# Reordering the step from the output projection to the gate/up products in a one-core encoder layer

## The chip, the core and the metric

The kernel runs on one core of a Trainium2 chip. The metric is the device time of one execution in microseconds. Five engines matter: PE (TensorE, the matrix products and transposes), ACT (ScalarE), DVE (VectorE), POOL (GpSimd) and SP (SyncE); the last two mostly issue DMA transfers. Each engine works through its own queue in the order in which the program wrote it, and waits at an instruction until the semaphores named there are reached.

## What is computed

One layer of a bidirectional encoder on 512 tokens of width 2048, all in float32. The part of it around the change is the end of the mixer, the second RMSNorm and the first half of the feed-forward block:

```
mixed = concat([attn_out, gla_out]) @ w_out
x = x + mixed
h = rmsnorm(x, ffn_norm_w)             # x * rsqrt(mean(x*x) + eps) * w
x = x + (silu(h @ w_gate) * (h @ w_up)) @ w_down
return rmsnorm(x, final_norm_w)
```

`w_out` is 2048x2048; `w_gate` and `w_up` are 2048x5632; `w_down` is 5632x2048.

## The kernel before

Every float32 product is made of products of two rounded halves, a high part and a low part, so one tile product is several matmuls.

**Output projection.** A job per 512 output columns (c = 0 to 3) runs over 16 k-tiles and accumulates four PSUM banks, one for each 128 tokens (`run_job`, L303 to L305). Before the job of c it has the residual tiles x1[c] loaded. When the job ends, `evac_out(c)` (L1033) adds the banks to x1[c] on DVE (L1038); for c = 3 in eight adds of 256 columns, the left halves of all four banks first, then the right halves. The rest is a generator appended to the queue `urgent`: `rest()` for c < 3, `rest_last()` (L1060) for c = 3. Each call of `run_urgent` (L235) runs the first generator in that queue up to its next `yield`, so what stands between two yields is emitted at the place of the call, on all engines at once.

**What the generators do.** `weighted` (L358) transposes four 128x128 blocks on PE into one PSUM bank (L362), and ACT copies that bank out with the norm's weight (L364). `pair_operands` (L1009) makes the seven token operands of a pair of k-tiles from two such copies: four subtractions and additions on DVE (L1014, L1017), then seven casts on ACT (L1026) and seven subtractions on DVE (L1014). `keep` (L1044) squares x1 on ACT with a row sum (L409) and stores x1 to DRAM from POOL's queue (L1047). `rstd_of` (L318) turns the sums into the reciprocal root: a scale, ACT's Ln and Exp (L323, L324), and four small operations of DVE. `rows_of` (L330) spreads the root along the tokens by matmuls with a broadcast column (L334) and an ACT copy (L337).

**Gate/up products.** `Feed.run` (L1340) walks over units (one of w_gate or w_up, 256 columns) of four pieces each (four k-tiles, 512 KB of weights). A piece needs sums of weight blocks (DVE, L1208 to L1211), a low part of the raw blocks (ACT L1186, then an accumulating DMA of POOL, L1187; the high part is L1188), and the split of the sums (ACT L1225, DVE L1226). They are emitted one to three pieces ahead, by `split`, `sums` and `part`. `products` (L1249) then multiplies: seven products (two matmuls each, one for each of the piece's pairs of k-tiles) of 512 columns with the high weights (L1278), then fourteen of 256 columns with the low weights (L1284). Products 0 to 5 accumulate over the unit in three double banks `pd`; product 6 in a single bank of the two called `pe`. The other `pe` bank is what the transposes and the rows get. Those are the eight PSUM banks, and they are the ones that the output projection has just used: a `pd` tile can be written once the adds have read the old banks under it. After a unit's last piece `empty` (L1296) reads each bank with ACT (L1305) and DVE (L1306), and `combine` (L1309) needs the rows for a gate unit (L1327).

The pieces of the first unit (i = 0 to 3) use k-tiles 0 to 15; those of c = 3 are only needed by piece 3. So `rest_last` is spread over pieces 0 to 3 by calls of `run_urgent` in `products` (L1282, L1287) and in `run` (L1346, L1356).

Of the kernel before, what the change touches and what calls it, by code (L numbers as in the profile page):

```python
# [19 lines left out]
OP = mybir.AluOpType  # L20
# [100 lines left out]
def layer(nc, tc, x, attn_norm_w, w_in, rel_table, gw_f, gb_f, gw_b, gb_b, gla_norm_w, w_out,  # L121
# [7 lines left out]
    with tc.manual_schedule(), \  # L129
# [851 lines left out]
        x1 = {}  # L981
# [50 lines left out]

        def evac_out(c):  # L1033
            def f(banks):
                for h in range(2 if c == 3 else 1):
                    a = slice(h * 256, (h + 1) * 256) if c == 3 else slice(0, 512)
                    for t in range(4):
                        dve.tensor_tensor(x1[c][t].t[:, a], x1[c][t].t[:, a], banks[t].t[:, a], op=OP.add)  # L1038
                put(*banks)
                if c < 3:  # L1040
                    load_res(c + 1)
                urgent.append(rest() if c < 3 else rest_last())

            def keep():  # L1044
                for t in range(4):
                    squares(c, t, x1[c], ss2)
                    pool.dma_start(out=xd[4 * c + t], in_=x1[c][t].t)  # L1047

            def rest():
                yield  # L1050
                keep()
                fs_ = {}
                for q in (2 * c, 2 * c + 1):
                    fs_[q] = [weighted(x1[c], k, W_FFN) for k in (2 * q, 2 * q + 1)]
                    yield
                put(*x1.pop(c))
                for q in (2 * c, 2 * c + 1):
                    yield from pair_operands(q, fs_.pop(q))

            def rest_last():  # L1060
                fs_ = {}
                for q in (2 * c, 2 * c + 1):
                    fs_[q] = []
                    for k in (2 * q, 2 * q + 1):
                        fs_[q].append(weighted(x1[c], k, W_FFN))
                        yield
                for q in (2 * c, 2 * c + 1):
                    yield from pair_operands(q, fs_.pop(q))
                keep()
                put(*x1.pop(c))  # L1070
                yield
                dve.tensor_reduce(sum2, ss2.rearrange("p (t c) -> p t c", c=4), op=OP.add,
                                  axis=mybir.AxisListType.X)
                rstd_of(sum2, 4, rstd2, 1.0 / D, scr)
                yield
                rb[2] = rows_of(rstd2)
            return f

# [79 lines left out]
        class Feed(Blocks):  # L1158
# [90 lines left out]
            def products(self, i, more):  # L1249
                st_ = self.sets.pop(i)  # L1250
                u, piece = self.seq[i]
                first, last = piece == 0, piece == self.per - 1
                (rh, rl), (sh, sl) = st_
                if first:
                    self.bank = {}
                if last:
                    groups = ((0, 1), (2, 3), (4, 5), (6,))
                elif first:
                    groups = (tuple(range(7)),)
                else:  # L1260
                    groups = ((0, 1, 5, 2, 3, 4, 6),)
                for group in groups:
                    todo = []
                    for n in group:
                        kind, xn = self.ORDER[n]
                        k = int(kind[1])
                        wh, wl = (rh, rl) if kind[0] == "R" else (sh, sl)
                        if first:
                            if n == 6:
                                self.bank[n] = ps.get()  # L1270
                                self.bank[6, 0] = self.bank[n].t
                            elif n % 2 == 0:
                                d = self.bank[n] = pd.get(F32, [P, 2, 512])
                                self.bank[n, 0], self.bank[n + 1, 0] = d.t[:, 0], d.t[:, 1]
                        o = self.bank[n, 0]
                        for p in range(2):
                            x_ = xs[2 * piece + p][xn]
                            mm(o, wh.t[:, p, k], x_.t.rearrange("p s t -> p (s t)"), start=first and p == 0,  # L1278
                               stop=False, skip_group_check=True)
                            todo.append((o, wl, p, k, x_))  # L1280
                        if i == 0 and n > 4:
                            run_urgent()  # L1282
                    for m, (o, wl, p, k, x_) in enumerate(todo):
                        mm(o[:, 256:512], wl.t[:, p, k], x_.t[:, 0], start=False, stop=last and p == 1,  # L1284
                           skip_group_check=True)
                        if i == 0 and m in (5, 11):
                            run_urgent()  # L1287
                    if last:
                        self.empty(group[0])
                        next(more, None)  # L1290
                        if group[0] == 2:
                            self.part(i + 3)
                for hi, lo in st_:
                    put(hi, lo)
# [45 lines left out]
            def run(self):  # L1340
                for i, (u, q) in enumerate(self.seq):
                    self.load()
                    self.split(i)
                    while 2 * q + 1 not in xs:
                        run_urgent()
                    for _ in range(3 if i in (1, 2) else 0):  # L1346
                        run_urgent()
                    self.sums(i + 1)
                    more = self.sum_steps(i + 2)
                    if q == 0:  # L1350
                        next(self.making, None)
                    else:
                        next(more, None)
                    self.split(i + 1)
                    if i > 3:
                        run_urgent()  # L1356
                    if q < 3:
                        for _ in more:
                            pass
                        if q < 2:  # L1360
                            next(self.making, None)
                        self.part(i + 3)
                        if q == 1:
                            next(self.making, None)
                    if q == 2 and self.sent:
                        put(self.sent)
                        self.sent = None
                    self.products(i, more)
                    if u == len(self.units) - 1:
                        for p in (2 * q, 2 * q + 1):  # L1370
                            put(*xs.pop(p).values())
                        down_start(q)
                    if q == self.per - 1:
                        self.making = self.combine(u)
# [408 lines left out]
```

## Time and profile before

| what | value |
|---|---|
| runs, median (lowest to highest) | 2214.81 us (2214.68 to 2216.66), 3 runs |
| the profiled execution | 2214.19 us, its span 2212.4 us |
| PE busy | 2186.4 us, 99% of the span |
| granted TensorE clock, mean over the span | 0.998 |
| HBM read, written | 246.58 MB, 46.20 MB |
| mean DMA rate | 170 GB/s |

The span is the time from the first to the last instruction of the core; the profiled execution's own time is 1.8 us longer. Start times of rows are counted from the span's start. In a row of the timeline, the first number is the start, the second the length from the start of the first to the end of the last of the instructions that it merges, and the bracket the idle time of the engine before it with what ended it. Matmuls overlap, so a merged row reaches beyond the start of the next one: what PE really takes for a group is the distance between starts.

### The profile page before, as it was taken

How to read it: one execution, taken by the hardware profiler on the slowest of the kernel's cores; microseconds unless marked ns; L12 is line 12 of the kernel's file. 1: busy time of each engine (PE TensorE's matmuls, PEld its weight loads, DVE VectorE, ACT ScalarE, POOL GpSimd, SP SyncE). 2: the span in 40 equal slices, each digit the busy share in tenths (PEclk: the TensorE clock that was granted, in tenths of full speed). 3: DMA queues.
4: the chain of work that ended last, by engine and by line, in shares of the span. 5: the costliest groups of instructions: out<-in, count | busy, mean ns of one | idle time of the engine just before them, and what ended most of it. 6: DMA issues, size and time to landing. Idle time of an engine off the chain costs nothing.

```text
span 2212.4 us, 33114 instructions
## 1 busy us (share of the span) xinstructions
PE 2186.4 (99%) x12374; PEld 1910.5 (86%) x12374; DVE 1565.0 (71%) x2724; ACT 1189.3 (54%) x1990; POOL 326.2 (15%) x349
## 2 busy tenths in 40 slices
PE   9999999999999999999999999999999999999998
PEld 7888888888888887888888888888888899999986
DVE  4366665754455346788888888888888897888777
ACT  5344444444445345666666666666666655555443
POOL 0000000000000011222222222222222200122220
PEclk9999999999999999999999999999999999999999
DMA  6525625242325433888889898898888865687892
GB/s 208 160 72 151 177 81 141 84 133 57 97 66 171 134 105 84 204 193 208 204 194 209 194 212 197 200 210 196 212 193 208 254 185 177 179 199 182 230 370 78
DMA packets 260274, 376.75 MB, mean 170 GB/s; under 512 B 18288, under 2 KB 179744, under 8 KB 260113
## 3 DMA queue, kind: packets, MB, share of 16 engines
q1 hardware_dynamic: 192800, 259.37, 37.6%
q0 software_dynamic: 66128, 114.21, 27.6%
q8 instruction: 97, 1.59, 0.3%
q10 hardware_dynamic: 1184, 1.06, 0.1%
q14 instruction: 65, 0.52, 0.1%
HBM read 246.58 MB, written 46.20 MB: 132 GB/s over the span
## 4 chain that ended last, share of the span: by engine, by line
PE 92%; DVE 3%; DMA 2%; ACT 1%; issue 1%; ACTq 0%; SPq 0%; POOL 0%; POOLq 0%; DVEq 0%
PE pd L1278 21%; PE pd L1284 11%; PE ps L303 5%; PE ps L304 5%; PE ps L305 5%; PE ps L295 5%; PE ps L297 5%; PE ps L296 5%; PE pu L1544 4%; PE pu L1542 4%; PE pu L1543 4%; PE pe L1278 4%; PE pe L1284 2%; PE ps L529 1%; PE pu L304 1%
## 5 line engine op out<-in xcount | busy, mean ns | idle before, releaser
L1278 PE MATMUL pd<-a,b 128*128 128x512 f32 x2112 | 529.6, 393 | 2.4 <-DVE a L1038 1.6
L1278 PEld LDWEIGHTS pd<-a,b 128*128 128x128 f32 x2112 | 380.4, 189 | 69.2 <-issue 2.0
L1284 PEld LDWEIGHTS pd<-a,b 128*128 128x128 f32 x2112 | 288.5, 190 | 21.4
L1284 PE MATMUL pd<-a,b 128*128 128x256 f32 x2112 | 294.9, 282 | 0.0
L202 DVE TENSOR_TENSOR a<-b,a 128x512 fp32r<-128x512 f32 x288 | 193.0, 687 | 138.6 <-ACT a L201 137.2
L1187 POOL DMA_DIRECT2D b<-b x176 | 209.7, 1248 | 535.6 <-ACT b L1186 410.3
L1225 ACT CAST b<-b 128x1024 fp32r<-128x1024 f32 x176 | 185.3, 1053 | 164.1 <-DVE b L1211 136.0
L1544 PE MATMUL pu<-b,a 128*128 128x256 f32 x896 | 255.1, 285 | 6.5 <-DVE a L1507 5.5
L1542 PE MATMUL pu<-b,a 128*128 128x256 f32 x896 | 254.5, 284 | 0.0
L1543 PE MATMUL pu<-b,a 128*128 128x256 f32 x896 | 254.4, 284 | 0.0
L1226 DVE TENSOR_TENSOR b<-b,b 128x1024 fp32r<-128x1024 f32 x176 | 214.9, 1221 | 51.5 <-ACT b L1225 27.7
L201 ACT CAST a<-b 128x512 fp32r<-128x512 f32 x288 | 169.7, 617 | 67.2 <-PE ps L305 22.3
L1544 PEld LDWEIGHTS pu<-b,a 128*128 128x128 f32 x896 | 172.8, 193 | 7.3 <-DVE a L1507 6.2
L1542 PEld LDWEIGHTS pu<-b,a 128*128 128x128 f32 x896 | 172.9, 193 | 0.0
L1543 PEld LDWEIGHTS pu<-b,a 128*128 128x128 f32 x896 | 172.9, 193 | 0.0
L1147 ACT CAST b<-b 128x768 fp32r<-128x768 f32 (+1 forms) x128 | 115.2, 947 | 84.8 <-PE pu L1544 27.4
L1306 DVE TENSOR_TENSOR a<-pd,a 128x512 f32<-128x512 f32 x132 | 91.4, 692 | 95.6 <-ACT a L1305 95.5
L1186 ACT ACTIVATE b<-b 128x768 fp32r<-128x768 f32 x176 | 149.2, 848 | 7.4 <-PE ps L305 5.6
L1152 DVE TENSOR_TENSOR b<-b,b 128x768 fp32r<-128x768 f32 (+1 forms) x128 | 134.4, 1086 | 20.0 <-ACT b L1147 20.0
L1188 ACT CAST b<-b 128x768 fp32r<-128x768 f32 x176 | 145.3, 825 | 0.6 <-PE ps L305 0.6
L1305 ACT COPY a<-pd 128x512 f32<-128x512 f32 x132 | 77.4, 587 | 102.0 <-PE pd L1284 102.0
L1208 DVE TENSOR_TENSOR b<-b 128x512 f32<-128x512 f32 x176 | 120.5, 685 | 0.0
(246 smaller groups left out, 4332.8 us busy)
## 6 DMA issues: line engine op xcount, KB each, us to landing
b<-b POOLq DMA_DIRECT2D x176, 384.0 KB, 5.4
b<-in_w_gate_dram SPq DMA_DIRECT2D x88, 512.0 KB, 4.2
b<-in_w_up_dram SPq DMA_DIRECT2D x88, 512.0 KB, 4.5
b<-in_w_down_dram SPq DMA_DIRECT2D x88, 512.0 KB, 5.6
b<-in_w_in_dram SPq DMA_DIRECT2D x48, 512.0 KB, 3.9
b<-in_w_in_dram SPq DMA_DIRECT2D x94, 256.0 KB, 4.5
b<-in_w_out_dram SPq DMA_DIRECT2D x32, 512.0 KB, 4.9
md<-a POOLq DMA_DIRECT2D x56, 256.0 KB, 8.3
```

The lines of the kernel that those rows point to most:

```text
L201: act.copy(h[2].t, r)
L202: dve.tensor_tensor(h[3].t, r, h[2].f, op=OP.subtract)
L1186: act.activation(lo.t, r, AF.Copy, scale=-1.0)
L1187: pool.dma_start(out=lo.f, in_=r, accum_op=OP.add)
L1188: act.copy(hi.t, r)
L1225: act.copy(hi.t, self.S[i].t)
L1226: dve.tensor_tensor(lo.t, self.S[i].t, hi.f, op=OP.subtract)
L1278: mm(o, wh.t[:, p, k], x_.t.rearrange("p s t -> p (s t)"), start=first and p == 0, stop=False, skip_group_check=True)
L1284: mm(o[:, 256:512], wl.t[:, p, k], x_.t[:, 0], start=False, stop=last and p == 1, skip_group_check=True)
L1542: mm(o, xh[:, t], wh, start=first and h == 0, stop=False, skip_group_check=True)
L1543: mm(o, xh[:, t], wl, start=False, stop=False, skip_group_check=True)
L1544: mm(o, xl[:, t], wh, start=False, stop=last, skip_group_check=True)
```

## The change

The last chunk's residual is added in four adds of 512 columns, a bank each, and each bank is given back after its add. `rest_last` begins with the squares, the store, the sums and the root, in one step; then it makes two transposes and their pair of operands, and again two and a pair; `rows_of` comes last. In the first piece of the first unit, products 0 to 5 get their high and low matmuls first, and the seventh product is opened behind them. The calls of `run_urgent` move: one ahead of the products of piece 0, two within its low matmuls, three ahead of piece 1, two after the second and third product of piece 1, three ahead of piece 2 and one after the second product of piece 2.

```diff
         def evac_out(c):
             def f(banks):
-                for h in range(2 if c == 3 else 1):
-                    a = slice(h * 256, (h + 1) * 256) if c == 3 else slice(0, 512)
-                    for t in range(4):
-                        dve.tensor_tensor(x1[c][t].t[:, a], x1[c][t].t[:, a], banks[t].t[:, a], op=OP.add)
-                put(*banks)
+                for t in range(4):
+                    dve.tensor_tensor(x1[c][t].t, x1[c][t].t, banks[t].t, op=OP.add)
+                    put(banks[t])
...
             def rest_last():
-                fs_ = {}
-                for q in (2 * c, 2 * c + 1):
-                    fs_[q] = []
-                    for k in (2 * q, 2 * q + 1):
-                        fs_[q].append(weighted(x1[c], k, W_FFN))
-                        yield
-                for q in (2 * c, 2 * c + 1):
-                    yield from pair_operands(q, fs_.pop(q))
                 keep()
-                put(*x1.pop(c))
-                yield
                 dve.tensor_reduce(sum2, ss2.rearrange("p (t c) -> p t c", c=4), op=OP.add,
                                   axis=mybir.AxisListType.X)
                 rstd_of(sum2, 4, rstd2, 1.0 / D, scr)
                 yield
+                for q in (2 * c, 2 * c + 1):
+                    fs_ = []
+                    for k in (2 * q, 2 * q + 1):
+                        fs_.append(weighted(x1[c], k, W_FFN))
+                        yield
+                    yield from pair_operands(q, fs_)
+                put(*x1.pop(c))
                 rb[2] = rows_of(rstd2)
...
+                if i == 0:
+                    groups = (tuple(range(6)), (6,))
...
-                        if i == 0 and n > 4:
+                        if (i, n) in ((1, 1), (1, 2), (2, 1)):
                             run_urgent()
...
-                        if i == 0 and m in (5, 11):
+                        if i == 0 and len(group) > 1 and m in (2, 5):
                             run_urgent()
...
-                    for _ in range(3 if i in (1, 2) else 0):
+                    for _ in range((1, 3, 3)[i] if i < 3 else 0):
                         run_urgent()
```

How the instructions stand now is shown at three places. The names are those of the program's buffers: `a_920` to `a_923` are the four residual tiles x1[3], `ps_311` to `ps_314` the last job's banks, `small` holds the sums and the root, `idn` is the identity. Line numbers behind the change are three to five lower (L1278 and L1284 become L1275 and L1281; L1225 and L1226 become L1220 and L1221; L1186 and L1188 become L1181 and L1183).

First place: DVE at the end of the last output job. Before, from the last weight split to the first operation on transposed operands:

```order
L1226 TENSOR_TENSOR b_271_7640<-b_268_7621,b_270_7639 128x1024
L1038 TENSOR_TENSOR a_920_7240<-a_920_7240,ps_311_7248 128x256
L1038 TENSOR_TENSOR a_921_7241<-a_921_7241,ps_312_7249 128x256
L1038 TENSOR_TENSOR a_922_7242<-a_922_7242,ps_313_7250 128x256
L1038 TENSOR_TENSOR a_923_7243<-a_923_7243,ps_314_7251 128x256
L1038 TENSOR_TENSOR a_920_7240<-a_920_7240,ps_311_7248 128x256
L1038 TENSOR_TENSOR a_921_7241<-a_921_7241,ps_312_7249 128x256
L1038 TENSOR_TENSOR a_922_7242<-a_922_7242,ps_313_7250 128x256
L1038 TENSOR_TENSOR a_923_7243<-a_923_7243,ps_314_7251 128x256
```

With the change:

```order
L1221 TENSOR_TENSOR b_271_7640<-b_268_7621,b_270_7639 128x1024
L1036 TENSOR_TENSOR a_920_7240<-a_920_7240,ps_311_7248 128x512
L1036 TENSOR_TENSOR a_921_7241<-a_921_7241,ps_312_7249 128x512
L1036 TENSOR_TENSOR a_922_7242<-a_922_7242,ps_313_7250 128x512
L1036 TENSOR_TENSOR a_923_7243<-a_923_7243,ps_314_7251 128x512
L1060 TENSOR_REDUCE small<-small 128x4
L322 TENSOR_SCALAR small<-small 128x4
L325 TENSOR_TENSOR small<-small 128x4
L326 TENSOR_TENSOR small<-small 128x4
L327 TENSOR_SCALAR small<-small 128x4
L328 TENSOR_TENSOR small<-small 128x4
```

The adds are four instead of eight, and the six small operations of the root, which stood 41 instructions further down, follow them directly. The first gate/up matmul writes `pd_1`, which lies over the bank `ps_313`: before it waits for the seventh add, now for the third.

Second place: PE in piece 0 of the first unit. Before, the first two groups of transposes (into `pe_1` and `pe_3`) with the seventh product (`pe_2`) between them:

```order
L362 MATMUL pe_1_7687<-idn,a_920_7240 128x128
L362 MATMUL pe_1_7687<-idn,a_921_7241 128x128
L362 MATMUL pe_1_7687<-idn,a_922_7242 128x128
L362 MATMUL pe_1_7687<-idn,a_923_7243 128x128
L1278 MATMUL pe_2_7694<-a_827_6651,b_258_7533 128x512
L1278 MATMUL pe_2_7694<-a_842_6728,b_258_7533 128x512
L362 MATMUL pe_3_7697<-idn,a_920_7240 128x128
L362 MATMUL pe_3_7697<-idn,a_921_7241 128x128
L362 MATMUL pe_3_7697<-idn,a_922_7242 128x128
L362 MATMUL pe_3_7697<-idn,a_923_7243 128x128
```

With the change, the second group of transposes (into `pe_2`) up to the seventh product (`pe_3`):

```order
L362 MATMUL pe_2_7716<-idn,a_920_7240 128x128
L362 MATMUL pe_2_7716<-idn,a_921_7241 128x128
L362 MATMUL pe_2_7716<-idn,a_922_7242 128x128
L362 MATMUL pe_2_7716<-idn,a_923_7243 128x128
L1281 MATMUL pd_2_7693<-a_826_6648,b_259_7534 128x256
L1281 MATMUL pd_2_7693<-a_841_6725,b_259_7534 128x256
L1281 MATMUL pd_3_7698<-a_822_6624,b_259_7534 128x256
L1281 MATMUL pd_3_7698<-a_837_6703,b_259_7534 128x256
L1281 MATMUL pd_3_7698<-a_828_6654,b_253_7375 128x256
L1281 MATMUL pd_3_7698<-a_843_6731,b_253_7375 128x256
L1275 MATMUL pe_3_7729<-a_827_6651,b_258_7533 128x512
L1275 MATMUL pe_3_7729<-a_842_6728,b_258_7533 128x512
```

Two groups of transposes now find a `pe` bank each, and the seventh product takes the first of these banks afterwards; the third and fourth group stand in piece 1 and share the bank that is left, and the rows' matmuls (L334) stand behind the second product of piece 2 instead of ahead of the sixth piece (the second unit's piece 1).

Third place: ACT between the second and the third group of transposes. Before, the reads of the four groups (L364) follow each other:

```order
L364 ACTIVATE a_978_7692<-pe_1_7687,wcol 128x512
L364 ACTIVATE a_979_7702<-pe_3_7697,wcol 128x512
L364 ACTIVATE a_980_7715<-pe_4_7710,wcol 128x512
L364 ACTIVATE a_981_7728<-pe_5_7723,wcol 128x512
L1026 CAST a_984_7738<-a_978_7692 128x256
L1026 CAST a_985_7741<-a_979_7702 128x256
```

With the change:

```order
L364 ACTIVATE a_983_7721<-pe_2_7716,wcol 128x512
L1026 CAST a_986_7740<-a_982_7711 128x256
L1026 CAST a_987_7743<-a_983_7721 128x256
L1026 CAST a_988_7746<-a_983_7721 128x256
L1026 CAST a_989_7749<-a_984_7734 128x256
L1026 CAST a_990_7752<-a_984_7734 128x256
L1026 CAST a_991_7755<-a_985_7735 128x256
L1026 CAST a_992_7758<-a_985_7735 128x256
L1181 ACTIVATE b_277_7768<-b_255_7408 128x768
L1183 CAST b_276_7767<-b_255_7408 128x768
L364 ACTIVATE a_993_7781<-pe_4_7776,wcol 128x512
```

Seven casts of the first pair and the two halves of a weight piece now stand between the second read and the third. The fourth group of transposes writes the bank that this third read empties. The four squares (L409) and the Ln and Exp of the root stand ahead of the first read, where they stood behind the operands of both pairs; the four stores of x1 stand three accumulating DMAs earlier in POOL's queue.

## The prediction on record

> **What bounds the kernel now.** I read the page's chain first, then the timeline of PE around the step, and last the windows with the granted clock.
>
> ```profile
> PE 92%; DVE 3%; DMA 2%; ACT 1%; issue 1%; ACTq 0%; SPq 0%; POOL 0%; POOLq 0%; DVEq 0%
> ```
>
> PE carries 92% of the chain that ended last. The change removes no matmul, so it can only win where PE waits or runs slowly. PE's timeline at the step (start, length, the merged group, idle time before it and what ended that):
>
> ```profile
> 866.86 0.39 PE L305 MATMUL ps<-a,b 128*128 128x512 f32 x1
> 868.85 3.01 PE L1278 MATMUL pd<-a,b 128*128 128x512 f32 x12 [1.60 <-DVE a L1038]
> 871.70 0.60 PE L362 MATMUL pe<-idn,a 128*128 128x128 f32 x4
> 872.05 0.71 PE L1278 MATMUL pe<-a,b 128*128 128x512 f32 x2
> 873.07 0.66 PE L362 MATMUL pe<-idn,a 128*128 128x128 f32 x4 [0.31 <-ACT a L364]
> ...
> 876.35 0.49 PE L1284 MATMUL pe<-a,b 128*128 128x256 f32 x2
> 876.67 2.91 PE L1278 MATMUL pd<-a,b 128*128 128x512 f32 x12
> ...
> 879.88 1.60 PE L1284 MATMUL pd<-a,b 128*128 128x256 f32 x12
> ...
> 881.55 2.91 PE L1278 MATMUL pd<-a,b 128*128 128x512 f32 x12
> ...
> 892.25 3.05 PE L1278 MATMUL pd<-a,b 128*128 128x512 f32 x12 [0.75 <-DVE a L1306]
> ...
> 899.49 1.13 PE L334 MATMUL pe<-idn,small 128*128 128x128 f32 x8 [2.06 <-DVE small L328]
> 900.38 4.58 PE L1278 MATMUL pd<-a,b 128*128 128x512 f32 x12
> ...
> 906.91 2.91 PE L1278 MATMUL pd<-a,b 128*128 128x512 f32 x12
> ```
>
> Distances between starts are what counts. An undisturbed piece takes 881.55 - 876.67 = 4.88: fourteen wide matmuls 879.88 - 876.67 = 3.21, so 0.23 each, and fourteen narrow ones 1.67, so 0.12 each. A group of four transposes takes 872.05 - 871.70 = 0.35, and the matmul behind it some 0.08 more (two narrow ones behind the last group take 876.67 - 876.35 = 0.32 instead of 0.24). Five losses show:
>
> - The first gate/up matmul starts 868.85 - 866.86 - 0.23 = **1.76** behind the end of the last w_out matmul.
> - Piece 0 takes 876.67 - 868.85 = 7.82, and 4.88 with four groups of 0.43 would be 6.60: **1.2** go into waits for ACT's reads of the one free `pe` bank, the first of them shown at 873.07.
> - The second unit starts at 892.25, two pieces after 881.55 would be 891.31: **0.94**.
> - The rows start at 899.49, a piece after 892.25 would be 897.13: **2.36**.
> - The piece behind the rows takes 906.91 - 900.38 = 6.53 without a wait, **1.65** too much.
>
> The windows explain the last (length; busy time of PE, PE's loads, DVE, ACT, POOL; granted clock; DMA):
>
> ```profile
> 866.84:870.25 3.41, 1.81 (x8) 1.22 (x7) 1.94 (x6) 0.00 (x0) 0.06 (x1) 1.00 0.66 115
> 897.56:900.97 3.41, 1.48 (x11) 1.42 (x12) 2.69 (x11) 1.94 (x5) 1.19 (x1) 1.00 0.27 46
> 900.97:904.39 3.42, 3.42 (x10) 2.65 (x9) 3.38 (x7) 3.39 (x4) 0.00 (x0) 0.50 0.95 133
> ```
>
> Right behind the wait for the rows the clock is halved for 3.41. In the 3.41 before that, PE was busy for 1.48; in the same length with the first wait in it, PE was busy for 1.81 and kept the full clock. So I read the wait for the rows as costing twice: 2.36 and 1.65.
>
> **The change part by part.** I walk PE through the new order with rows of DVE, of the adds' line, and of ACT:
>
> ```profile
> 866.61 0.42 DVE L1038 TENSOR_TENSOR a<-a,ps 128x256 f32<-128x256 f32 x1 [0.26 <-PE ps L305]
> 867.29 1.75 DVE L1038 TENSOR_TENSOR a<-a,ps 128x256 f32<-128x256 f32 x5 [0.26 <-PE ps L305]
> ...
> 897.71 0.16 DVE L1072 TENSOR_REDUCE small<-small 128x4 f32<-128x16 f32 x1
> ...
> 899.18 0.16 DVE L328 TENSOR_TENSOR small<-small 128x4 f32<-128x4 f32 x1
> ```
>
> ```profile
> L1038 DVE TENSOR_TENSOR a<-a,ps x20: 414/686/689, 729.3 to 868.6; 128x512 f32<-128x512 f32 x12, 128x256 f32<-128x256 f32 x8
> ```
>
> ```profile
> 872.33 0.69 ACT L364 ACTIVATE a<-pe,wcol 128x512 f32<-128x512 f32 x1 [6.19 <-PE pe L362]
> ...
> 876.63 0.69 ACT L364 ACTIVATE a<-pe,wcol 128x512 f32<-128x512 f32 x1 [0.75 <-PE pe L362]
> 877.22 2.23 ACT L1026 CAST a<-a 128x256 fp32r<-128x256 f32 x7
> 879.36 0.84 ACT L1186 ACTIVATE b<-b 128x768 fp32r<-128x768 f32 x1
> 880.11 0.82 ACT L1188 CAST b<-b 128x768 fp32r<-128x768 f32 x1
> ...
> 890.24 1.06 ACT L1305 COPY a<-pd 128x512 f32<-128x512 f32 x2
> ```
>
> *The adds.* A 512-column add takes 0.69 (the median of the line), and PE frees a bank every 867.29 - 866.61 = 0.68, so four of them keep pace. The third starts at 866.61 and ends at 867.30. Before, PE waited for the seventh of eight adds: the group of five ends with the eighth at 869.04, the seventh one step of 0.33 earlier at 868.71, and PE began 0.14 behind that. By the same delay it now begins at 867.45, **1.40 earlier**. The fourth add ends near 868.0, well ahead of its reader, the ninth matmul, at 869.3.
>
> *Piece 0.* From 867.45, twelve wide matmuls lead to 870.20 and three narrow ones to 870.56, the first group. The second follows at 870.56 + 0.43 + 0.36 = 871.35; it has a bank of its own. Group, overhead and six narrow matmuls lead to 872.50. The seventh product needs ACT's first read, which begins 872.33 - 871.70 = 0.63 behind its group and ends at 871.88: no wait. Four matmuls, 0.70, and piece 1 starts at 873.20.
>
> *Piece 1 has a new wait.* The third group stands at 873.20 + 0.92 = 874.12; with it, the overhead and four wide matmuls PE comes to the fourth group at 875.47. This one writes the bank that ACT's third read empties, and that read now stands behind seven casts and two weight halves. ACT's second read begins at 871.35 + 0.63 = 871.98; the casts 877.22 - 876.63 = 0.59 later; they take 879.36 - 877.22 = 2.14, the halves 880.11 - 879.36 = 0.75 and some 0.73. So the third read begins at 876.19 and ends at 876.88, and PE, with the delay of 0.05 seen at 873.07 (872.33 + 0.69), goes on at 876.93: a wait of **1.46**, with all later products behind it. Its bounds: nothing, if ACT's third read comes as soon behind its group as the first did (0.63, so 874.75 to 875.44), and 3.6, if the casts, which wait for DVE's subtractions in turn, take as long again. I take 1.46, since seven such casts in a row are what 877.22 shows. Behind it, a group from a standstill 0.41 (873.07 to the matmul behind it), six wide matmuls 1.38 and 0.08, fourteen narrow 1.67: piece 2 starts at 880.47; before it was 881.55. So of the 1.40 about **0.3 is lost**: one wait of 1.46 replaces three of 1.2 in all.
>
> *Root and rows.* Four squares, at most 0.69 each on ACT like its reads of that size, run behind the adds and end before 868.9; ACT was idle there for 6.19, which hides them. The root takes 899.18 + 0.16 - 897.71 = 1.63 and is there by 870.6. PE comes to the rows at 880.47 + 0.92 = 881.4: the wait goes and nothing is late in its place. The rows' own 900.38 - 899.49 = 0.89 and 0.08 move into piece 2. Piece 3 then starts at 886.32, before 886.43: **0.1** is left of the gain. The operands of piece 3 hang on the fourth read of ACT, near 878.3; fourteen casts and subtractions behind it, at about 0.31 each in turn, end near 882.7, 3.6 ahead. The squares' old place is the cover that the second unit lacked: ACT came to the bank copies only at 890.24.
>
> *Second unit.* The first double bank of the first unit is complete near 888.0; ACT copies it in 0.58 and DVE adds it in 0.69, so it is free at 889.4, before PE needs it. The second unit starts at 886.32 + 4.88 = 891.20 (before 892.25), its second piece at 896.08, its third, without rows, wait or half clock, at 900.96. Before, that was 906.91: **5.95 earlier**.
>
> *Stores and loads.* The four stores of x1 pass three accumulating transfers on POOL.
>
> ```profile
> b<-b POOLq DMA_DIRECT2D x176, 384.0 KB, 5.4
> ```
>
> The first of these starts behind ACT's half at about 870.5 and lands near 876; PE wants it in piece 3, at 887. POOL is covered by 11, and past that each us would be one of PE's. SP's order is unchanged; its next weight load waits for sums that DVE now ends sooner. The order of chunks 0 to 2 stays, too.
>
> **Sum**: first matmul 1.40, transposes -0.3, rows moved -0.97, makes 0.1 at piece 3; the second unit's late start 0.94; rows and their wait 0.89 + 2.36; half clock 1.65: 5.95. The profiled execution's own 2214.19 gives 2208.2. The median of the runs stands 0.6 above it, so the forecast for the median is **2208.9**, 4.3 of it from waits and 1.65 from the clock.
>
> **Rivals.**
>
> *The clock keeps its part (2210.6).* The new wait could halve the clock as the one for the rows did. Against: its window leaves PE busy for some 1.95, over the 1.81 that kept full clock; it tips if ACT is 0.4 later than reckoned. Or the windows lie elsewhere in other executions and the runs had no half clock at the rows to lose. Chance 0.20.
> [...]
>
> *ACT is quicker (2207.5).* The fourth group finds its bank free. Chance 0.05.
>
> *The gain is lost behind the step (2213 to 2215).* The weights come no sooner, and PE waits for them in units two and three. For: a DMA share of 0.95 at 900.97. Against: the loads hang on releases by ACT and DVE, which come sooner too, and no idle time shows on PE behind 906.91 with the same streams. Chance 0.15.
>
> *Slower (2219).* The same weight stream had the old waits as its slack; 5.95 come back as three waits of 2 each, and each leaves PE so little of a window that the clock is halved: 2214.2 + 3 x 1.65. It decides where a wait leaves less than about 1.6 busy in 3.41. Chance 0.05.
>
> *The rows still wait.* Only if the root came 11 late; no chance is set aside.
>
> **How the numbers follow.** The forecast holds 0.55. A change under 0.2%, 4.4 us, is about what a measurement of this kernel cannot tell from none, so faster means below 2210.4. There lie the forecast, the quick ACT and 0.08 of the clock's case: 0.68. The rest of that case and the lost gain make 0.27; slower is 0.05. The range runs from 2207.2, just under the quick ACT, to 2212.4, the clock's case with half a wait more; what is left outside has 0.2.
>
> **What would show it.** Right: a first L1278 matmul under 0.7 behind the last of w_out; the fourth group waiting about 1.4 for ACT; no wait at the rows; 0.3 at most ahead of the second unit; a granted clock of 1.00 from 866 to 910. Wrong: 0.50 in a window near 878, a wait over 2 in piece 1, or PE waiting for weights in the second unit.

## The result, and the profile after

| | median | lowest to highest | runs |
|---|---|---|---|
| before | 2215.01 us | 2214.68 to 2218.61 | 6 |
| changed | 2208.36 us | 2205.94 to 2210.67 | 6 |

The ratio is 0.9966, with a 95% interval of 0.9953 to 0.9979: the change saves 6.65 us of the medians (by the interval 4.7 to 10.4). The forecast was 2208.9. The changed kernel's profiled execution took 2210.67 us, its span 2208.9; it is the slowest of the six, and what it lost outside the step is shown further down.

To compare executions I use one length that lies wholly inside the trace, the **step**: from the start of the last w_out matmul to the first wide matmul of the second unit's third piece. Before the change it is 906.91 - 866.86 = 40.05. PE's timeline of the changed kernel at the same place (columns as in the prediction):

```profile
866.46 0.39 PE L305 MATMUL ps<-a,b 128*128 128x512 f32 x1
866.95 3.02 PE L1275 MATMUL pd<-a,b 128*128 128x512 f32 x12
...
870.96 0.60 PE L362 MATMUL pe<-idn,a 128*128 128x128 f32 x4
...
872.81 1.09 PE L1275 MATMUL pd<-a,b 128*128 128x512 f32 x4
...
874.09 1.17 PE L1275 MATMUL pd<-a,b 128*128 128x512 f32 x4
876.52 0.66 PE L362 MATMUL pe<-idn,a 128*128 128x128 f32 x4 [1.26 <-ACT a L364]
...
880.09 1.09 PE L1275 MATMUL pd<-a,b 128*128 128x512 f32 x4
881.02 1.05 PE L334 MATMUL pe<-idn,small 128*128 128x128 f32 x8
...
885.86 1.09 PE L1275 MATMUL pd<-a,b 128*128 128x512 f32 x4
...
890.78 2.89 PE L1275 MATMUL pd<-a,b 128*128 128x512 f32 x12
...
900.51 2.91 PE L1275 MATMUL pd<-a,b 128*128 128x512 f32 x12
```

The step is 900.51 - 866.46 = **34.05**, 6.00 shorter; the prediction had 5.95. One wait is left, the new one of the fourth group of transposes. The rows (881.02) and the second unit (890.78) start without one, and the granted clock, the first number behind the five engines in the windows, is full through the step:

```profile
866.00:910.00 44.00, 42.64 (x250) 37.11 (x249) 34.40 (x70) 33.26 (x60) 10.49 (x11) 1.00 0.67 159
```

The page's chain had PE at 92% and DVE at 3% before. Now it reads:

```profile
PE 90%; DVE 4%; DMA 4%; ACT 1%; issue 1%; SPq 0%; ACTq 0%; DVEq 0%
```

It says nothing of the change: 6 us are 0.3% of the span. Only the stretch itself shows them.

### The profile page after: what moved, and what is told of

Read it like the earlier page. It is cut to its first block, busy times and chain, and to the rows that moved or that the text cites. A ratio compares the mean times of both kernels' runs of the same rounds, so it can differ in the third digit from the quotient of the medians.

```text
span 2208.9 us, 33105 instructions
## 1 busy us (share of the span) xinstructions
PE 2185.1 (99%) x12374; PEld 1909.9 (86%) x12374; DVE 1564.8 (71%) x2720; ACT 1189.8 (54%) x1990; POOL 326.3 (15%) x349
## 3 DMA queue, kind: packets, MB, share of 16 engines
q8 instruction: 97, 1.59, 0.3%
## 4 chain that ended last, share of the span: by engine, by line
PE 90%; DVE 4%; DMA 4%; ACT 1%; issue 1%; SPq 0%; ACTq 0%; DVEq 0%
PE pd L1275 22%; PE pd L1281 11%; PE ps L303 5%; PE ps L305 5%; PE ps L304 5%; PE ps L295 5%; PE ps L297 5%; PE ps L296 5%; PE pe L1275 4%; PE pu L1541 3%; PE pu L1540 3%; PE pu L1539 3%; PE pe L1281 2%; DMA b<-in_w_down_dram 2%; PE ps L529 1%; DVE b L1147 1%
## 5 line engine op out<-in xcount | busy, mean ns | idle before, releaser
L1275 PE MATMUL pd<-a,b 128*128 128x512 f32 x2112 | 528.4, 392 | 0.1
L1275 PEld LDWEIGHTS pd<-a,b 128*128 128x128 f32 x2112 | 378.9, 188 | 66.3 <-DVE a L1036 0.5
L1281 PEld LDWEIGHTS pd<-a,b 128*128 128x128 f32 x2112 | 288.5, 190 | 21.6
L1281 PE MATMUL pd<-a,b 128*128 128x256 f32 x2112 | 294.9, 282 | 0.0
L1220 ACT CAST b<-b 128x1024 fp32r<-128x1024 f32 x176 | 185.4, 1053 | 166.6 <-DVE b L1206 138.4
L1221 DVE TENSOR_TENSOR b<-b,b 128x1024 fp32r<-128x1024 f32 x176 | 214.8, 1221 | 50.7 <-ACT b L1220 26.3
L1181 ACT ACTIVATE b<-b 128x768 fp32r<-128x768 f32 x176 | 149.2, 847 | 4.7 <-PE ps L305 2.9
L1183 ACT CAST b<-b 128x768 fp32r<-128x768 f32 x176 | 145.2, 825 | 0.6 <-PE ps L305 0.6
```

The lines of the kernel that those rows point to most:

```text
L1181: act.activation(lo.t, r, AF.Copy, scale=-1.0)
L1220: act.copy(hi.t, self.S[i].t)
L1221: dve.tensor_tensor(lo.t, self.S[i].t, hi.f, op=OP.subtract)
```

## The experiments

Line numbers differ by a few from kernel to kernel; the operations are the same. "Rows" are the L334 matmuls. All measured steps:

| kernel | step | time (us) |
|---|---|---|
| before, three profiles | 40.05, 40.42, 38.57 | median 2215.01 |
| changed, three profiles | 34.05, 34.04, 34.06 | median 2208.36 |
| e1: adds alone | 38.88 | 2215.64, one run |
| e2: root ahead alone | 35.04 | 2213.12, one run |
| e3: zeros into the rows' wait | 38.65 | 2214.43, one run |
| e4: all four groups in piece 0 | 32.67 | median 2207.45, 5 runs |
| e5: seventh product not last | 35.13 | 2214.06, one run |
| e6: rows later | 34.03 | 2206.50, one run |
| e7: half adds | 35.53 | 2209.44, one run |
| e8: e4, and zeros in two late waits | 32.65 | median 2205.18, 5 runs |

The theory is the prediction's sum, term by term; the main rival is that the half clock keeps its part. A single run's time tells little, as the last experiments show, so the verdicts go by the step.

**e1, the adds alone.** The kernel before with the new adds:

```diff
-                for h in range(2 if c == 3 else 1):
...
-                put(*banks)
+                for t in range(4):
+                    dve.tensor_tensor(x1[c][t].t, x1[c][t].t, banks[t].t, op=OP.add)
+                    put(banks[t])
```

> The kernel before with the last chunk added a bank at a time, nothing else. Measured by the step: from the start of the last w_out matmul to the first matmul of the second unit's third piece, 40.05 us before and 34.05 us with the whole change. Theory: PE waits for the third instead of the seventh add, the first gate/up matmul comes 1.4 us earlier and every later wait moves along, so the step takes 38.65. Rival: the waits behind it are set by ACT and DVE, whose work also hangs on the adds only in part, and swallow the gain: 39.5 to 40.05.

PE's timeline of e1, at the start of the step and at the rows:

```profile
867.79 0.39 PE L305 MATMUL ps<-a,b 128*128 128x512 f32 x1
868.28 3.02 PE L1276 MATMUL pd<-a,b 128*128 128x512 f32 x12
...
899.23 1.75 PE L334 MATMUL pe<-idn,small 128*128 128x128 f32 x8 [2.38 <-DVE small L328]
```

The first gate/up matmul starts 0.49 behind the start of the last w_out matmul, 1.50 earlier than the 1.99 of before. The step is 38.88, only 1.17 shorter: the wait for the rows is 2.38 here, where it was 2.06. The rows are released by the root, so PE's coming sooner can be swallowed there; but the unchanged kernel shows 2.43 for that wait in another execution (e9, a step of 40.42, against which e1 is 1.54 shorter), so this run can't say how much was.

**e2, the root ahead alone.** The kernel before with squares, store, sums and root at the start of `rest_last`; the adds and the transposes stay. Two yields fall away, so the rows move too, to a place ahead of the first unit's fourth piece (e6 tests what their place is worth).

```diff
             def rest_last():
+                keep()
+                dve.tensor_reduce(sum2, ss2.rearrange("p (t c) -> p t c", c=4), op=OP.add,
+                                  axis=mybir.AxisListType.X)
+                rstd_of(sum2, 4, rstd2, 1.0 / D, scr)
                 fs_ = {}
...
-                keep()
                 put(*x1.pop(c))
-                yield
...
-                yield
                 rb[2] = rows_of(rstd2)
```

> The kernel before with the squares, the store and the root ahead of the first transposes, and the rows at the end of the operands (they fall ahead of the first unit's fourth piece); adds, transposes and the seventh product as before. Theory: the wait for the rows (2.36), its half clock (1.65) and the second unit's late start (0.94) go, the first wait of 1.76 and the waits of the transposes (1.2) stay: the step takes 40.05 - 4.95 = 35.1. Rival, the half clock has another cause than this wait: 36.75. Rival, the squares ahead of the first read of ACT delay the transposes by up to 2.5: 37.6.

PE's timeline of e2, from the rows to the end of the step:

```profile
887.50 1.05 PE L334 MATMUL pe<-idn,small 128*128 128x128 f32 x8
...
893.28 2.89 PE L1276 MATMUL pd<-a,b 128*128 128x512 f32 x12
...
903.01 2.91 PE L1276 MATMUL pd<-a,b 128*128 128x512 f32 x12
```

The step falls by 5.01 to 35.04 (903.01 - 867.97). No group shown carries a wait, and 903.01 is 9.73 behind 893.28, two undisturbed pieces, and the granted clock is 1.00 from 866 to 910: no half clock. The prediction's terms for this part were 2.36, 0.94 and 1.65, in all 4.95. So, against the first profile of before, the root's place alone is worth five sixths of the change. Against e10, the execution of the kernel before without a half clock at the rows, it is 38.57 - 35.04 = 3.53 of 4.52.

**e3, the clock alone.** The kernel before, with nine matmuls on a tile of zeros ahead of the rows (`spin`, which the kernel has for its first microseconds; the trace records each as two). Their results are not read; nothing of the computation is left out.

```diff
                 yield
+                spin(9)
                 rb[2] = rows_of(rstd2)
```

> The kernel before with nine added matmuls on zeros (128 columns, about 2 us in all) ahead of the rows' matmuls, so that PE is busy while it waits for the root; nothing is read from them. Theory, the idle share of a 3.41 us window halves the clock: the rows start at the same place, the piece behind them takes 4.88 instead of 6.53, clock 1.00, the step takes 40.05 - 1.65 = 38.4. Rival, the half clock comes from something else in this stretch: 40.05 and 0.50 as before.

PE's timeline of e3:

```profile
897.97 2.17 PE L890 MATMUL pe<-warm 128*128 128x128 f32 x18
900.40 1.13 PE L334 MATMUL pe<-idn,small 128*128 128x128 f32 x8 [0.26 <-DVE small L328]
901.29 2.99 PE L1279 MATMUL pd<-a,b 128*128 128x512 f32 x12
...
906.25 2.91 PE L1279 MATMUL pd<-a,b 128*128 128x512 f32 x12
```

The rows come no sooner (900.40 is 32.80 behind the start of the last w_out matmul at 867.60; before it was 32.63), but the piece behind them takes 906.25 - 901.29 = 4.96 instead of 6.53, and the step is 1.40 shorter. So the loss behind the rows was one of clock, not of weights. One execution alone would not show that the zeros keep the clock, since e10 keeps it without them; but with them PE idles only 0.26 there, so every 3.41 across this wait leaves it busy for 3.15 or more, where the stretch that lost the clock had 1.48.

**e4, all four groups in piece 0.** The changed kernel with its third and fourth group of transposes moved from piece 1 into piece 0, ahead of both pairs' operands, so that no read of ACT stands behind casts.

```diff
-                    fs_ = []
+                    fs_[q] = []
...
-                    yield from pair_operands(q, fs_)
+                for q in (2 * c, 2 * c + 1):
+                    yield from pair_operands(q, fs_.pop(q))
...
-                        if (i, n) in ((1, 1), (1, 2), (2, 1)):
+                        if (i, n) == (2, 1):
...
-                        if i == 0 and len(group) > 1 and m in (2, 5):
+                        if i == 0 and len(group) > 1 and m in (2, 5, 7, 10):
```

> The changed kernel with all four groups of transposes in piece 0 (behind the 3rd, 6th, 8th and 11th narrow matmul), alternating over the two pe banks, and the operands of both pairs behind them. Theory: the wait of 1.43 in piece 1 comes from the third read of ACT standing behind seven casts and two weight halves; with the four reads in a row it goes, at most 0.1 appears ahead of the seventh product: the step takes 34.05 - 1.4 = 32.65, and the time falls by 1.4 against the changed kernel. Rival: the reads, 0.69 each, are themselves the bound, and the transposes wait for banks by about 1.2 again: 33.9.

PE's timeline of e4, around the fourth group:

```profile
872.36 0.60 PE L362 MATMUL pe<-idn,a 128*128 128x128 f32 x4
...
873.74 2.91 PE L1277 MATMUL pd<-a,b 128*128 128x512 f32 x12
```

The wait of piece 1 is gone, and the step 1.38 shorter at 32.67. That is the price of the new wait in the changed kernel. Five runs have a median of 2207.45 (2205.75 to 2208.34), 0.996 of the kernel before on that chip (0.9947 to 0.9974).

**e5, the seventh product back in its place.** The changed kernel without the order that opens the seventh product last in piece 0.

```diff
-                if i == 0:
-                    groups = (tuple(range(6)), (6,))
```

> The changed kernel with the seventh product back among the first seven of piece 0, so that it holds one pe bank from the start; all else as changed. Theory: the second group of transposes then waits for ACT's read of the first, 0.56 by the rows of before, and the rest moves along: the step, 34.05 us with the whole change, takes 34.6. Rival: the wait in piece 1 shrinks by as much, since it ends with ACT: 34.05.

PE's timeline of e5:

```profile
870.26 0.61 PE L1273 MATMUL pe<-a,b 128*128 128x512 f32 x2
...
872.45 0.66 PE L362 MATMUL pe<-idn,a 128*128 128x128 f32 x4 [0.42 <-ACT a L364]
...
878.07 0.66 PE L362 MATMUL pe<-idn,a 128*128 128x128 f32 x4 [1.70 <-ACT a L364]
```

The step is 35.13, 1.08 longer than the changed kernel's, twice what was expected. The seventh product holds one `pe` bank from 870.26, so the second group waits 0.42 for ACT to empty the other, and it starts 872.45 - 866.92 = 5.53 into the step (866.92 is the last w_out matmul's start), where in the changed kernel it is 870.96 - 866.46 = 4.50. The expectation had only the part from group to group, 872.45 - 871.07 = 1.38 against 870.96 - 870.16 = 0.80, so 0.58; the other 0.45 is PE's time for the seventh product's two wide matmuls, which now stand ahead of the first group. Everything of ACT up to the third read hangs on that group, and the fourth group waits for the third read: 878.07 - 866.92 = 11.15 against 876.52 - 866.46 = 10.06. The delay of 1.03 goes through to the end, because the fourth group waits for ACT in any case. Opening the seventh product last is worth 1.08.

**e6, the rows later.** The changed kernel with two more steps of the generator ahead of the rows.

```diff
                 put(*x1.pop(c))
+                yield
+                yield
                 rb[2] = rows_of(rstd2)
```

> The changed kernel with the rows' matmuls back behind the second unit's first piece, where they stood before; the root stays early. Theory: the wait there was for the root and not for the place, so the rows go through without a wait, 0.9 of matmuls only change their piece and the step stays at 34.05; clock 1.00. Rival: the place is what counts, a bank or the ACT queue is late there too: 35.5 or more.

PE's timeline of e6 at the rows, which now stand behind the first piece of the second unit as before the change:

```profile
894.27 0.40 PE L1283 MATMUL pe<-a,b 128*128 128x256 f32 x2
894.50 1.05 PE L334 MATMUL pe<-idn,small 128*128 128x128 f32 x8
```

No wait, and a step of 34.03. That the rows were built in the third piece has no part in the gain: it is the root's place that took the wait away.

**e7, the half adds.** The changed kernel with the eight adds of before: e1's diff read backwards.

> The changed kernel with the last chunk added in eight half-width adds as before. Theory: PE waits for the seventh add again and every step behind it moves along, since the squares and the root hang on the same adds: 34.05 + 1.5 = 35.55. Rival: the wait of 1.4 in piece 1 takes up the delay, as ACT's queue there does not depend on PE's start: 34.4.

PE's timeline of e7:

```profile
866.59 0.39 PE L305 MATMUL ps<-a,b 128*128 128x512 f32 x1
868.57 3.00 PE L1277 MATMUL pd<-a,b 128*128 128x512 f32 x12 [1.60 <-DVE a L1038]
```

The old wait of 1.60 is back, and the step is 35.53, 1.48 longer: with the root ahead, the whole gain of the adds reaches the end of the step.

**e8, zeros in two late waits.** PE waits twice for DVE in the down projection, 1.8 near 1920 and 3.6 near 2025, in the kernel before and in the changed one alike. This is e4 with matmuls on zeros in front of these two places; their results are not read.

```diff
+                    if n == 2 and i in (28, 48):
+                        spin(8 if i == 28 else 15)
                     for h in range(2):
                         o = self.banks[n].t[:, h * 256:(h + 1) * 256]
```

> The kernel with four groups in piece 0 (step 32.67, median 2207.45), and added matmuls on zeros at two waits of the later w_down products, eight in the one of 1.84 near 1917 and fifteen in the one of 3.64 near 2021; nothing is read from them. Theory, a 3.41 window with PE busy for less than about half halves the clock of the next: the halved stretches behind both waits go (clock 1.00 at 1919 and 2025), 1.65 each where they were: about 2204.5, and a smaller spread, since the place of the windows no longer matters there. Rival, matmuls on zeros don't count as activity, or the added ones lengthen the path by what they save: 2207.5.

PE's timeline of e8 at the second place:

```profile
2019.84 3.51 PE L890 MATMUL pu<-warm 128*128 128x128 f32 x30
```

And its windows around both places:

```profile
1900.00:1940.00 40.00, 38.93 (x321) 38.32 (x321) 36.18 (x60) 22.46 (x34) 6.10 (x7) 1.00 0.74 198
2010.00:2060.00 50.00, 49.72 (x415) 49.35 (x414) 40.66 (x62) 27.01 (x38) 14.48 (x18) 1.00 0.84 206
```

Five runs have a median of **2205.18**, from 2204.98 to 2205.80, 0.9954 of the kernel before on that chip (0.994 to 0.9967). That is the lowest median tried. The waits are still there as time, filled; what goes is the half clock behind them: the mean granted clock in these two windows is 1.00, where e4's profile has 0.96 and 0.97. The spread is 0.8 instead of the 2.6 of e4, which fits, with five runs each. How much the zeros bring is not settled: e4 and e8 ran on two chips, and the intervals of their ratios overlap.

**e9 to e12, the same two kernels in other executions.** The kernel before twice (e9, e10) and the changed one twice (e11, e12), unchanged, to see whether the half clock belongs to a wait or to where the wait falls.

> The kernel before, unchanged, in another execution. Theory: the clock is granted in stretches of 3.41 us on a raster whose place differs between executions, and a stretch is halved where PE was busy for under about 1.63 us (between the 1.58 that halved and the 1.69 that did not) of the one ahead. The matmuls stand as in the first profile (step 40.05 with a half clock at the rows, 38.4 without it; a wait of 2.06 ahead of the rows, 1.84 near 1920). Slid along the first profile, the raster halves the clock behind the rows for 56% of its places and behind the wait near 1920 for 50%. So in each of the two executions one or the other may be missing, the step is 40.05 or 38.4, and which it is follows from the place of the raster. Rival: the half clock belongs to the rows' wait as such: 40.05 in both executions, whatever the raster.

> As the run before it: step 40.05 where the stretch of 3.41 us that holds the rows' wait leaves PE under 1.63 us, 38.4 where it leaves more. Rival: 40.05 whatever the raster.

> The changed kernel, unchanged, in another execution. Theory: step 34.05 and full clock from 866 to 910 again, since no place of the raster leaves PE under 2.1 us there; the half clock near 1921 is there where the stretch ahead of it leaves PE under 1.63 us (half of the places), and the time is about 1.7 lower without it; the wait of 1.64 near 2141, which the kernel before did not show, is a matter of the single execution and need not come again. Rival: both are part of what the change costs and come in every execution.

> As the run before it: step 34.05, full clock from 866 to 910; near 1921 and 2141 as the raster has it.

The windows of e10, cut where the clock's stretches begin (length; busy time of PE, PE's loads, DVE, ACT, POOL; granted clock; DMA):

```profile
897.29:900.70 3.41, 1.49 (x11) 1.43 (x12) 2.70 (x11) 1.94 (x5) 1.19 (x1) 1.00 0.25 42
900.70:904.12 3.42, 3.42 (x20) 2.95 (x19) 3.38 (x7) 3.39 (x4) 0.00 (x0) 1.00 0.95 137
1921.29:1924.70 3.41, 1.57 (x13) 1.37 (x12) 3.41 (x5) 1.17 (x2) 1.75 (x2) 1.00 0.41 104
1924.70:1928.11 3.41, 3.41 (x17) 3.41 (x18) 2.65 (x7) 1.77 (x3) 1.16 (x2) 0.50 1.09 193
```

And those of e9 at the rows:

```profile
896.60:900.01 3.41, 0.98 (x9) 0.81 (x8) 2.73 (x9) 1.86 (x4) 0.59 (x1) 1.00 0.44 76
900.01:903.42 3.41, 3.41 (x11) 2.83 (x11) 3.34 (x7) 2.67 (x3) 0.61 (x1) 0.50 0.73 98
```

PE's timeline of e10 behind the rows:

```profile
899.22 1.13 PE L334 MATMUL pe<-idn,small 128*128 128x128 f32 x8 [2.18 <-DVE small L328]
900.10 2.98 PE L1278 MATMUL pd<-a,b 128*128 128x512 f32 x12
...
905.04 2.91 PE L1278 MATMUL pd<-a,b 128*128 128x512 f32 x12
```

In e10 the rows wait 2.18, and yet the clock stays full behind them; the piece takes 905.04 - 900.10 = 4.94, and the step is 38.57. In e9 the wait is 2.43 and the clock is halved: 40.42. So the rival, a half clock that belongs to the rows' wait as such, falls. But the limit that the expectation put falls too. By 1.63 of busy time e10 should have lost its clock: its stretch has 1.49, all but the same as the 1.48 of the first profile, which did. And in the same e10, 1.57 with the down projection's matmuls did halve it.

The windows of the changed kernel's first profile, in the step's wait and near 1920:

```profile
873.23:876.65 3.42, 2.16 (x12) 1.46 (x12) 3.38 (x10) 3.24 (x7) 1.18 (x1) 1.00 0.27 45
...
1917.71:1921.12 3.41, 1.57 (x13) 1.37 (x13) 3.38 (x7) 1.05 (x3) 1.75 (x2) 1.00 0.73 162
1921.12:1924.53 3.41, 3.41 (x18) 3.41 (x18) 3.26 (x6) 3.11 (x6) 1.72 (x2) 0.50 1.05 180
```

And those of e12, at its start and near 1920, where the wait of the same length lies otherwise in the raster:

```profile
8.21:11.62 3.41, 3.40 (x12) 3.10 (x13) 1.44 (x2) 1.31 (x2) 0.00 (x0) 0.50 1.05 337
...
1919.68:1923.09 3.41, 1.75 (x14) 1.75 (x15) 3.38 (x8) 1.05 (x3) 1.62 (x3) 1.00 0.86 186
1923.09:1926.50 3.41, 3.41 (x31) 3.41 (x30) 3.21 (x5) 3.41 (x7) 2.26 (x3) 1.00 1.06 169
```

These explain what the first profile lost outside the step. It has a half clock at 1921.12: from the matmul behind the wait near 1920 to the one behind the next long wait it takes 2026.10 - 1919.99 = 106.11, where e11 and e12 take 104.76, so 1.35. And it has a longer wait late, in the timeline of PE:

```profile
2142.93 0.47 PE L303 MATMUL pu<-a,a 128*128 128x512 f32 x1 [1.64 <-DVE a L1419]
```

e11 has no half clock near 1920 and idles only 0.71 ahead of the same matmul (2140.46 there), and took 2208.20. e12 has neither; it took 2210.24 for two other reasons. Its clock was halved at 8.21, and its step begins at 867.81 instead of 866.46. And two stretches in a row are halved behind its long wait, from 2025.49 to 2032.32, where e11 has one: from there to the matmul behind the next wait it takes 2123.43 - 2026.11 = 97.32, e11 2120.62 - 2024.73 = 95.89. None of these lies in the step, which is 34.04 to 34.06 in all three. For the other five of the six runs there is no profile.

## Why the prediction was right

The forecast, 2208.9, is 0.5 above the median, and each sign that it had named came: the first matmul, the new wait, the rows, the second unit and the full clock. That the median is so close is in part luck: the term for the clock was too large for the average execution, and the medians differ by more than the step does, for a cause left open below. Its walk through the step against the first profile, in lengths from start to start:

| stretch | reckoned | measured |
|---|---|---|
| last w_out to first gate/up matmul | 0.59 | 866.95 - 866.46 = 0.49 |
| piece 0 | 5.75 | 872.81 - 866.95 = 5.86 |
| piece 1 | 7.27 | 880.09 - 872.81 = 7.28 |
| piece 2, with the rows | 5.85 | 885.86 - 880.09 = 5.77 |
| piece 3 | 4.88 | 890.78 - 885.86 = 4.92 |
| second unit, two pieces | 9.76 | 900.51 - 890.78 = 9.73 |
| in all | 34.10 | 34.05 |

- **The adds** (1.40 reckoned): 1.50 by e1, 1.48 of the step by e7. The four adds keep pace, as the groups of before had let expect; DVE's timeline of the changed kernel has them in one piece, 4 x 0.68 long, and the root's last operation ends at 870.00, 11 ahead of the rows at 881.02, as counted:

```profile
864.84 2.73 DVE L1036 TENSOR_TENSOR a<-a,ps 128x512 f32<-128x512 f32 x4 [2.11 <-PE ps L305]
...
869.84 0.16 DVE L328 TENSOR_TENSOR small<-small 128x4 f32<-128x4 f32 x1
```

- **The new wait in piece 1** (1.46 reckoned): from 874.09, four wide matmuls of 0.23 and the overhead of 0.08 lead to 875.09, and the group starts at 876.52, so 1.43. ACT's timeline shows the chain that was reckoned, seven casts, two weight halves, then the third read:

```profile
872.18 2.24 ACT L1026 CAST a<-a 128x256 fp32r<-128x256 f32 x7
874.32 0.85 ACT L1181 ACTIVATE b<-b 128x768 fp32r<-128x768 f32 x1
875.06 0.82 ACT L1183 CAST b<-b 128x768 fp32r<-128x768 f32 x1
875.79 0.68 ACT L364 ACTIVATE a<-pe,wcol 128x512 f32<-128x512 f32 x1
```

  The read was reckoned to begin at 876.19 in the forecast's times, in which the step starts 0.40 later (866.86 instead of 866.46): that makes 875.79 here, as measured. e4 shows the wait from the other side: without it the step is 1.38 shorter.
- **Rows, second unit and their wait** (2.36 and 0.94): no wait at either in any run with the root ahead (e2, e4, e6 and the changed kernel).
- **The half clock** (1.65): this is the term that was mis-sized, for the median. The first profile of before had it, and against that profile it was right. But of the three profiles of before, the first lost 6.53 - 4.88 = 1.65 there, e9 906.77 - 900.40 - 4.88 = 1.49 and e10 0.06. So over executions it is worth about 1.1, and the rival that spoke of runs without a half clock at the rows described one execution in three. By the mean of the three profiles the step shrank by 39.68 - 34.05 = 5.63.
- **The limit for the clock** (a stretch with PE busy for 1.48 is followed by half clock, one with 1.81 isn't) was taken from two rows, and it is not sharp: e10 kept its clock with 1.49 and lost it with 1.57 elsewhere. The forecast didn't hang on it, since the new wait left more than that in the stretch that holds it: 2.16 behind 873.23 in the first profile, 2.15 in e11 and e12. Of the stretches read here, those with 0.08 (first profile before, ahead of 2030.78) to 1.59 of PE's time busy (e9) were followed by half clock, e10's 1.49 being the one exception, and with the wait filled (e3, 3.15 or more) or gone (e2) it didn't come. Where a stretch begins differs from execution to execution: the rows start at 899.49 in the first profile before and at 899.33 in e9, the half clock behind them at 900.97 and at 900.01.
- **The gain lost behind the step, and slower by the weight stream**: neither came. From the end of the step to the matmul behind the next wait, near 1911, the first profile of the changed kernel takes 1911.06 - 900.51 = 1010.55 and that of before 1917.46 - 906.91 = 1010.55; the other two profiles of each agree within 0.01. What the step gained arrives there whole.

What stays open: 6.65 of the medians against 5.63 of the step. The difference lies within the interval, and single executions differ by as much through the places of the clock's stretches (1.35 near 1920, in the first profile of the changed kernel against e11 and e12); it isn't attributed. The mean spans of the three profiles of each kernel, 2213.1 and 2207.9, differ by 5.2. Nor is it settled what decides about the clock between 1.48 and 1.69 of busy time (e10's two stretches differ in the kind of matmul too, 512 and 256 columns).

## What to carry to other kernels

Where small work sits between two dense stretches, issue the longest dependent chain first (here sums and root, on engines that were idle) and what only feeds a distant reader later: that gave 5.0 of 6.0 (3.5 of 4.5 against an execution without the half clock), while moving the reader itself gave nothing. Ask of each bank which engine empties it, and what stands ahead of that read in the engine's queue; e4 shows that a copy of 0.7 behind casts of other data cost 1.4, e5 that a product opened early in one of two banks cost 1.1. Waits of PE of 1.83 to 2.43 cost more in clock in some executions (1.65 and 1.49 behind the rows, 1.35 near 1920) and next to nothing in others (0.06 behind the rows in e10). Where such a wait can't be removed, matmuls on zeros can stand in it: they kept the full clock here (e3: 4.96 for the piece behind it instead of 6.53; e8: 1.00 in both windows); the median went from 2207.45 to 2205.18 with them (e4 to e8; by the ratios to the kernel before 1.3, which is not clear of the noise).

## What had not been expected of the hardware

In these traces the granted clock changes on a raster, a regular grid in time, whose place differs from execution to execution. In the first profile before, halved stretches of 3.41 begin at 900.97 and at 2030.78, in e9 at 900.01 and at 2033.24: 1129.81 and 1133.23 apart, which is 331 and 332 times 3.4133. In the changed kernel's first profile they begin at 1921.12 and at 2026.93, 105.81 or 31 times 3.4133 apart. A wait of 1.83 to 1.85 near 1920, the same in every execution, was followed by half clock in the changed kernel's first profile (1.57 of PE's time busy in the stretch ahead), in e10 (1.57), e5 (1.58) and e9 (1.59), and not in e12 (1.75), e11 (2.00), the first profile before (1.99) or e7, which had 1.69:

```profile
1918.07:1921.48 3.41, 1.69 (x15) 1.48 (x13) 3.41 (x6) 1.17 (x2) 1.75 (x2) 1.00 0.35 79
1921.48:1924.90 3.42, 3.31 (x27) 3.31 (x28) 3.32 (x9) 2.40 (x4) 1.65 (x2) 1.00 1.02 193
```

So two executions of one kernel differ by 1.35 at a place that no edit touched. e5's single time of 2214.06, against a step 1.08 longer than the changed kernel's, is the plainest case; it too has the half clock behind the wait near 1920, and its windows behind the longer wait show two such stretches in a row:

```profile
2027.59:2034.42 6.83, 5.48 (x25) 5.48 (x26) 4.34 (x8) 3.52 (x6) 1.72 (x2) 0.50 0.94 182
```

There 5.48 of PE's time ran at half speed, where the changed kernel's first profile has one stretch of 3.41: to the matmul behind the next wait e5 takes 2125.91 - 2028.94 = 96.97, the first profile 2122.17 - 2026.10 = 96.07, so 0.90 more, about as much as the seventh product's place cost. In these runs the way back to the full clock took more of PE's time than staying there, for which 1.69 was enough in e7: halved stretches with PE busy for 2.06 (e5) and 2.79 (e12) were followed by a second one, those with 3.05 (e11) and 3.13 (first profile before) were not. A difference of 2 us between single times of this kernel means nothing without the windows.
